# A gated MLP on one core: three single gate loads and their matmuls ahead of all value columns, and one output block stored whole

## The chip, the core and the metric

The kernel runs on one core of one Trainium2 chip. A core has five engines that run side by side: TensorE (PE; its weight loads are listed apart as PEld), VectorE (DVE), ScalarE (ACT), GpSimd (POOL) and SyncE (SP). SP issues most of the DMAs; ACT and POOL can issue DMAs too. Each engine works through its own list of instructions in order, and waits on semaphores where an instruction needs another engine's result or a DMA's landing.

The metric is the device time of one execution in microseconds (us). Lower is better.

## The reference

```python
batch, seq, dim, hidden = 16, 256, 512, 2048
x  = randn(batch, seq, dim)      # 4096 rows of 512, float32
w1 = randn(dim, hidden * 2)      # gate columns, then value columns
w2 = randn(hidden, dim)

def reference(x, w1, w2):
    h = x @ w1
    gate, value = split(h, 2, axis=-1)
    h = maximum(gate, 0) * value
    return (h @ w2).astype(float32)
```

So there are two large matrix products, with a product of the positive part of the gate and the value between them.

## The kernel before

**Stages.** The 4096 rows of x are worked in four sets of 1024 (`SET`), each set in two halves of 512 (`TH`). The hidden dimension of 2048 is cut into 16 blocks of 128 (`jb`, 0 to 15). For each set, the first matrix product makes `g`, the gated hidden values in fp16, block by block, and the second product (`mm2_stream`) multiplies `g` with w2. Both products use a scheme with seven products of halves (`P1` to `P7` in class `Block` and in `mm2_stream`) in place of eight; sums of halves of x, w1, g and w2 are made for it on DVE and POOL. The order of instructions on every engine is the order in which the program emits them (`manual_schedule`); no scheduler changes it.

**The start.** The sums of w1 aren't there yet when the first set starts. So the first three blocks (`NPLAIN = 3`) are computed plainly, by class `Plain`: four matmuls for the gates (`gates`), four for the values (`values`), and `close`, which scales the values on ACT (L269) and multiplies them with the positive part of the gates on DVE (L270). For the first 512 rows (`whole`) a block is one piece of 512 columns; for the second 512 rows (`parts`) it is two pieces of 256.

All that the plain blocks need is loaded by SP in one queue, in the order of the program (L418 to L425): the first 512 rows of x in two loads into `xf`, the gate columns of blocks 0 and 1 in one load, their value columns in one load, rows 512 to 767 of x (`xg[:2]`), the gate columns of block 2, its value columns, and rows 768 to 1023 (`xg[2:]`). `fetch_wl(jb, g_, n)` loads `n` blocks of columns of one kind (`g_` 0 is gate, 1 is value) in float32: 256 KB a block, in rows of 512 bytes a block. `cast_w(jb, g_)` turns one block's columns into fp16 in `wr`, half on ACT and half on DVE (both L401). The loads land in space that belongs to `g` and its sums, so that they cost no memory of their own.

x has to be transposed ahead of the matmuls. `turn_pair` does it for the first 512 rows, in float32, by matmuls with an identity on PE (L383), copied out by DVE (even row blocks) and ACT (odd ones) (L385). The second 512 rows are cast to fp16 on DVE first (`xh`, L459 and L469), then turned by `turn_half` on PE (L391) and copied out on DVE (L392).

**Other work that hangs on these loads.** POOL issues the loads of all other w1 columns, in fp16, and its first one waits behind a small copy (L428) that reads the value columns of block 0: a gate that holds POOL's loads back until those have landed. DVE's first sum of w1 (`w1_one`, L160) needs POOL's first two loads, and `lead`, the first block with seven products (block 3), needs those sums. All SP and ACT loads take their completion semaphores from a ring of eight, so a load waits until the one eight places earlier has landed.

**The end.** In the last set (`last`) the second product's output goes out by block of 128 rows, `b` from 0 to 3, for each half of the set's rows. The upper rows' output `o1` (L324) is stored whole for blocks 0 and 1 and as two halves of 256 columns for blocks 2 and 3. The lower rows' output `o2` is stored in halves for blocks 2 and 3 (L330, L338), and the very last half is issued by ACT (L335).

Of the kernel before, what the change touches and what calls it, by code (L numbers as in the profile page):

```python
# [21 lines left out]
NPLAIN = 3  # L22
# [3 lines left out]
HALF = 256  # L26
# [3 lines left out]
@with_exitstack  # L30
def kernel(ctx: ExitStack, tc: tile.TileContext, x, w1, w2, out):

    nc = tc.nc
    x2 = x.flatten_outer_dims()
    out2 = out.flatten_outer_dims()  # L40
    flagpool = ctx.enter_context(tc.tile_pool(name="flagpool", bufs=1))
    flag = flagpool.tile([1, 1], dt.int32, name="flag")
    with ExitStack() as fast:
        unfit = fast_way(fast, tc, x2, w1, w2, out2, flag)
    with tc.If(unfit > 0, label="general"):
        with ExitStack() as general:
            general_way(general, tc, x2, w1, w2, out2)
# [52 lines left out]
def fast_way(ctx, tc, x2, w1, w2, out2, flag):  # L100
# [4 lines left out]
    H, DO = w2.shape  # L105
# [13 lines left out]
    psy = ctx.enter_context(tc.tile_pool(name="psy", bufs=3, space=bass.MemoryType.PSUM))  # L119
# [164 lines left out]
    def mm2_stream(s, go):  # L284
        last = s == NS - 1
        S = {}

        def mm(name, b, ps, fresh):
            vn, gn = WX[name]
            for k in range(NHC):  # L290
                nc.tensor.matmul(ps, go[gn][:, k, b * P:(b + 1) * P], V[vn][:, k, :], start=fresh and k == 0,  # L291
                                 stop=k == NHC - 1, skip_group_check=True)
                if k < NHC - 1:
                    yield

        def take(pool, nm):
            return pool.tile([P, TH], F32, name=nm, tag=nm)[:, :HALF]

        def step(name, b):
            d = S.setdefault(b, {})  # L300
            if name == "P1":
                d["X"] = take(psx, "X")
                yield from mm("P1", b, d["X"], True)
                d["Y"] = take(psy, "Y")
                nc.scalar.copy(out=d["Y"], in_=d["X"])
            elif name == "P5":
                d["W"] = take(psw, "W")
                yield from mm("P5", b, d["W"], True)
                t = tmp.tile([P, 2, TH], F32, name="pv", tag="tmp")
                d["pu"], d["o2"] = t[:, 0].rearrange("p (a n) -> p a n", a=2), t[:, 1]  # L310
                nc.scalar.activation(d["pu"][:, 0], d["W"], COPY, scale=1 / GS)
            elif name == "P2":
                yield from mm("P2", b, d["X"], False)
                d["o1"] = tmp.tile([P, DO], F32, name="o", tag="o", bufs=4)
                nc.scalar.activation(d["o1"][:, :HALF], d["X"], COPY, scale=1 / GS)
            elif name == "P6":
                yield from mm("P6", b, d["Y"], False)
                nc.scalar.activation(d["pu"][:, 1], d["Y"], COPY, scale=-1 / GS)
            elif name == "P3":
                yield from mm("P3", b, d["W"], False)  # L320
                nc.vector.scalar_tensor_tensor(out=d["o1"][:, HALF:], in0=d["W"], scalar=1 / GS, in1=d["pu"][:, 1],  # L321
                                               op0=MULT, op1=ADD)
                for n in (slice(0, HALF), slice(HALF, DO)) if last and b >= 2 else (slice(0, DO),):
                    nc.sync.dma_start(out=out_v[s, 0, b, :, n], in_=d["o1"][:, n])  # L324
            elif name == "P7":
                yield from mm("P7", b, d["Y"], False)
                nc.vector.scalar_tensor_tensor(out=d["o2"][:, HALF:], in0=d["Y"], scalar=-1 / GS, in1=d["pu"][:, 0],
                                               op0=MULT, op1=ADD)
                if last and b >= NB - 2:
                    nc.sync.dma_start(out=out_v[s, 1, b, :, HALF:], in_=d["o2"][:, HALF:])  # L330
            else:
                yield from mm("P4", b, d["Y"], False)
                nc.scalar.activation(d["o2"][:, :HALF], d["Y"], COPY, scale=1 / GS)  # L333
                if last and b == NB - 1:
                    nc.scalar.dma_start(out=out_v[s, 1, b, :, :HALF], in_=d["o2"][:, :HALF])  # L335
                else:
                    n = slice(0, HALF if last and b == NB - 2 else DO)
                    nc.sync.dma_start(out=out_v[s, 1, b, :, n], in_=d["o2"][:, n])  # L338
            yield

        order = [("P1", 0), ("P1", 1), ("P1", 2), ("P2", 0), ("P2", 1), ("P2", 2)]
        order += [(n, b) for n in ("P5", "P6", "P3", "P7", "P4") for b in (0, 1)]
        order += [("P1", 3), ("P5", 2), ("P2", 3), ("P5", 3)]
        order += [(n, b) for n in ("P6", "P3", "P7", "P4") for b in (2, 3)]
        for i, (n, b) in enumerate(order):
            for f in BESIDE.get((s, i), ()):
                f()
            yield from step(n, b)
# [38 lines left out]
    def turn_half(o, b0, copy):  # L387
        ps = psx.tile([P, 4, 2, P], F16, name="X", tag="X")
        for b in range(2):
            for e in range(4):  # L390
                nc.tensor.transpose(ps[:, e, b], xh[:, b0 + b, e * P:(e + 1) * P], ident[F16])  # L391
        copy(out=o["A2"][:, :, b0 * P:(b0 + 2) * P], in_=ps.rearrange("p e b t -> p e (b t)"))  # L392
# [5 lines left out]
    def cast_w(jb, g_):  # L398
        c, i = place[jb]
        for es, copy in ((slice(0, 2), nc.scalar.copy), (slice(2, 4), nc.vector.tensor_copy)):  # L400
            copy(out=wr[c][:, es, g_, i * P:(i + 1) * P], in_=wl[c][:, es, g_, i * P:(i + 1) * P])  # L401

    def fetch_wl(jb, g_, n=1):
        c, i = place[jb]
        nc.sync.dma_start(out=wl[c][:, :, g_, i * P:(i + n) * P], in_=w1_v[:, :, g_, jb * P:(jb + n) * P])
# [11 lines left out]

    for b in (0, 2):  # L418
        nc.sync.dma_start(out=xf[:, b:b + 2], in_=x_v[0, :, b:b + 2])  # L419
    fetch_wl(0, 0, 2)  # L420
    fetch_wl(0, 1, 2)
    nc.sync.dma_start(out=xg[:, :2], in_=x_v[0, :, NB:NB + 2])
    fetch_wl(2, 0)
    fetch_wl(2, 1)
    nc.sync.dma_start(out=xg[:, 2:], in_=x_v[0, :, NB + 2:])  # L425
    for t in ident.values():
# [7 lines left out]
    whole = [Plain(g, jb, xo["A1"], 0, 0, 2) for jb in range(NPLAIN)]  # L434
# [19 lines left out]
    cast_w(1, 0)  # L454
    whole[0].gates((1,))
    whole[1].gates(None, psy, "Y")
    cast_w(0, 1)
    cast_w(1, 1)
    nc.vector.tensor_copy(out=xh[:, :2], in_=xg[:, :2])  # L459
    whole[0].values()  # L460
    whole[0].close()
    whole[1].values()
    cast_w(2, 0)
    turn_half(xo, 0, nc.vector.tensor_copy)
    whole[2].gates(None, psy, "Y")
    cast_w(2, 1)
    whole[1].close()
    whole[2].values()
    nc.vector.tensor_copy(out=xh[:, 2:], in_=xg[:, 2:])  # L469
# [69 lines left out]
    for s in range(NS):  # L539
# [7 lines left out]
        last = NJ * PERIOD  # L547
# [16 lines left out]
        for at in range(first * PERIOD, last + PERIOD):  # L564
            if at in plan:
                jb, n = plan[at]
# [87 lines left out]
```

## Time and profile before

| what | value |
|---|---|
| median of 3 runs | 309.1 us (309.0 to 309.37) |
| the profiled execution's own time | 309.1 us |
| span of its profile, first to last instruction | 307.3 us |
| mean granted TensorE clock | 0.999 |
| DMA, mean over the span | 103 GB/s |
| longest groups on PE: L205 (first product, seven products) X, Y, W | 379 ns a matmul of 128x512 |
| PE L291 (second product) | 273 ns a matmul of 128x256 |

A line of the timeline reads: start and duration in us, engine, line of the kernel, operation, out<-in by the program's names, size, number of instructions that were merged, and in square brackets the idle time of the engine just ahead and what ended it. The name of a tile is that of the memory it lies in: `g_S<-in_x_dram` is a load of x, `g<-in_w_dram` one of the first three blocks' columns, and `wr<-g` their cast. An "q" behind an engine's name is its queue: an instruction that issues a DMA. Matmuls are pipelined, so a group's end overlaps the next one's start: it is the distance of the starts that counts.

### The profile page before, as it was taken

Reading aid. Unit: us, or ns where it says so; the run is one execution under the profiler, and the core shown is the slowest. Engines: PE = TensorE matmul, PEld = TensorE weight load, DVE = VectorE, ACT = ScalarE, POOL = GpSimd, SP = SyncE. Lnnn points to the kernel's source line nnn. Section 1 sums busy time; section 2 is a strip of 40 time slices with the busy share of each in tenths; the row PEclk is TensorE's granted clock in tenths of the full one; section 3 lists DMA queues with packets and bytes.
Section 4 is the critical chain, followed back from the end, with each engine's and each line's share of the span. In section 5 each row is a group of like instructions: output and inputs, shape, how many; then the busy total and the mean of one; then the engine's idle time right before and its main releaser. Section 6 shows DMA issues by size and latency. Waiting matters only on the chain.

```text
span 307.3 us, 5116 instructions
## 1 busy us (share of the span) xinstructions
PE 300.6 (98%) x1868; PEld 182.7 (59%) x1868; DVE 219.1 (71%) x346; ACT 189.8 (62%) x457; POOL 139.7 (45%) x127
## 2 busy tenths in 40 slices
PE   7999999999999999999999999999999999999994
PEld 4574444588844444488864444458884444448883
DVE  1798898896568888884348888885526888888401
ACT  2557776568576676737856767656857767673230
POOL 1749999810004438990002345994000433898000
PEclk9999999999999999999999999999999999999999
DMA  6999986989615740065130010036321100000123
GB/s 227 305 204 205 207 203 192 183 155 186 237 61 102 140 102 1 2 119 155 69 139 24 11 34 2 0 69 140 138 80 59 34 9 27 0 2 0 69 88 124
DMA packets 34410, 31.54 MB, mean 103 GB/s; under 512 B 14448, under 2 KB 28784, under 8 KB 34160
## 3 DMA queue, kind: packets, MB, share of 16 engines
q1 hardware_dynamic: 24608, 20.32, 21.9%
q0 software_dynamic: 9104, 10.75, 21.3%
q8 instruction: 15, 0.25, 0.4%
q10 hardware_dynamic: 672, 0.13, 0.2%
q14 instruction: 11, 0.09, 0.1%
HBM read 24.12 MB, written 11.53 MB: 116 GB/s over the span
## 4 chain that ended last, share of the span: by engine, by line
PE 96%; DMA 2%; ACT 0%; SPq 0%; issue 0%; ACTq 0%
PE Y L205 26%; PE X L205 17%; PE W L205 17%; PE Y L291 14%; PE W L291 9%; PE X L291 9%; DMA g<-in_w_dram 2%; PE W L255 2%; PE X L255 1%; PE Y L255 1%; SPq L419 0%; PE X L391 0%; ACT Y L212 0%; ACT wr L401 0%; ACT pv L333 0%
## 5 line engine op out<-in xcount | busy, mean ns | idle before, releaser
L280 POOL TENSOR_TENSOR g_S<-g 128x512 f16<-128x512 f16 (+1 forms) x46 | 58.1, 1292 | 126.3 <-DVE g L244 126.3
L205 PEld LDWEIGHTS <-wt 128*128 128x128 f16 x488 | 47.7, 98 | 55.9 <-issue 0.3
L205 PE MATMUL X<-x_A,wr 128*128 128x512 f16 x244 | 72.6, 379 | 0.1
L205 PE MATMUL Y<-x_S,wt 128*128 128x512 f16 x244 | 72.6, 379 | 0.0
L205 PEld LDWEIGHTS <-wr 128*128 128x128 f16 x366 | 35.8, 98 | 41.4 <-issue 0.4
L232 DVE SCALAR_TENSOR_TENSOR cc<-W,pu 128x512 f32<-128x512 f32 x61 | 42.2, 691 | 24.2 <-ACT pu L226 24.2
L212 ACT COPY Y<-X 128x512 f32<-128x512 f32 x61 | 34.8, 570 | 38.0 <-PE X L205 37.5
L291 PEld LDWEIGHTS <-g_S 128*128 128x128 f16 x512 | 50.0, 98 | 5.8
L238 DVE SCALAR_TENSOR_TENSOR cc<-Y,pu 128x512 f32<-128x512 f32 x61 | 42.2, 691 | 6.2
L226 ACT ACTIVATE pu<-Y 128x512 f32<-128x512 f32 x61 | 36.4, 596 | 13.8 <-PE Y L205 13.8
L233 DVE SCALAR_TENSOR_TENSOR g<-X,cc 128x512 f16<-128x512 f32 x61 | 42.2, 691 | 2.4
L244 DVE SCALAR_TENSOR_TENSOR g<-Y,cc 128x512 f16<-128x512 f32 x61 | 41.5, 681 | 1.8 <-PE Y L205 1.8
L291 PEld LDWEIGHTS <-g 128*128 128x128 f16 x384 | 37.6, 98 | 8.2
L219 ACT ACTIVATE pu<-W 128x512 f32<-128x512 f32 x61 | 36.7, 602 | 0.3 <-PE W L205 0.3
L205 PE MATMUL Y<-x_A,wt 128*128 128x512 f16 x122 | 36.3, 379 | 0.0
L205 PE MATMUL W<-x_S,wr 128*128 128x512 f16 x122 | 36.3, 379 | 0.0
L205 PE MATMUL W<-x_S,wt 128*128 128x512 f16 x122 | 36.3, 379 | 0.0
L291 PE MATMUL X<-w,g 128*128 128x256 f16 x256 | 31.2, 273 | 0.0
L291 PE MATMUL Y<-v,g_S 128*128 128x256 f16 x256 | 30.6, 273 | 0.0
L321 DVE SCALAR_TENSOR_TENSOR o<-W,pv 128x256 f32<-128x256 f32 x16 | 6.8, 424 | 29.2 <-PE W L291 29.2
L280 POOL TENSOR_TENSOR g_S<-g,g_S 128x512 f16<-128x512 f16 x18 | 21.8, 1209 | 1.4
L280 POOL TENSOR_TENSOR g_S<-g_S,g 128x512 f16<-128x512 f16 x18 | 20.8, 1154 | 1.4
(76 smaller groups left out, 285.7 us busy)
## 6 DMA issues: line engine op xcount, KB each, us to landing
out_dram<-o SPq DMA_DIRECT2D x14, 256.0 KB, 2.1
out_dram<-pv SPq DMA_DIRECT2D x14, 256.0 KB, 2.0
x<-in_x_dram POOLq DMA_DIRECT2D x3, 1024.0 KB, 9.4
xn<-x SPq DMA_DIRECT2D x12, 256.0 KB, 3.0
g_S<-in_x_dram SPq DMA_DIRECT2D x4, 512.0 KB, 6.5
wr<-in_w_dram POOLq DMA_DIRECT2D x4, 512.0 KB, 13.0
w<-in_w_dram POOLq DMA_DIRECT2D x4, 512.0 KB, 15.4
g<-in_w_dram SPq DMA_DIRECT2D x2, 512.0 KB, 6.5
```

Source lines behind the costliest of these rows:

```text
L205: nc.tensor.matmul(ps, W(wn, self.jb)[:, b], self.xo[xn][:, b, :], start=fresh and b == 0, stop=b == 1, skip_group_check=True)
L212: nc.scalar.copy(out=self.Y, in_=self.X)
L219: nc.scalar.activation(self.p5, self.W, COPY, scale=GS)
L226: nc.scalar.activation(self.u2, self.Y, COPY, scale=-GS)
L232: nc.vector.scalar_tensor_tensor(out=self.c12, in0=self.W, scalar=GS, in1=self.u2, op0=MULT, op1=ADD)
L233: nc.vector.scalar_tensor_tensor(out=self.g[:, self.jb, :TH], in0=self.X, scalar=0.0, in1=self.c12, op0=MAX, op1=MULT)
L238: nc.vector.scalar_tensor_tensor(out=self.c22, in0=self.Y, scalar=-GS, in1=self.p5, op0=MULT, op1=ADD)
L244: nc.vector.scalar_tensor_tensor(out=self.g[:, self.jb, TH:], in0=self.Y, scalar=0.0, in1=self.c22, op0=MAX, op1=MULT)
L255: nc.tensor.matmul(ps[:, ts], W(names[e // 2], self.jb)[:, e % 2], self.a[:, e, ts], start=e == 0, stop=e == 3, skip_group_check=True)
L280: eng.tensor_tensor(go[n][:, h0:h1], go[i0][:, h0:h1], go[i1][:, h0:h1], op=op)
L291: nc.tensor.matmul(ps, go[gn][:, k, b * P:(b + 1) * P], V[vn][:, k, :], start=fresh and k == 0, stop=k == NHC - 1, skip_group_check=True)
L321: nc.vector.scalar_tensor_tensor(out=d["o1"][:, HALF:], in0=d["W"], scalar=1 / GS, in1=d["pu"][:, 1], op0=MULT, op1=ADD)
```

## The change

It has three parts. In the loads, the pair of gate columns (blocks 0 and 1) becomes two single loads, and the gate columns of block 2 follow at once as a third, ahead of the value columns of blocks 0 and 1; before, they came after the rows 512 to 767 of x. In the order of the work, the cast and the gate matmuls of block 2 move ahead of the casts of the values of blocks 0 and 1, and the cast of block 2's values moves ahead of the first `turn_half`, where the cast of block 2's gates was. At the end, the upper output of block 2 is stored whole; only block 3's is stored in halves.

```diff
@@ in mm2_stream
-                for n in (slice(0, HALF), slice(HALF, DO)) if last and b >= 2 else (slice(0, DO),):
+                for n in (slice(0, HALF), slice(HALF, DO)) if last and b >= 3 else (slice(0, DO),):
                     nc.sync.dma_start(out=out_v[s, 0, b, :, n], in_=d["o1"][:, n])
@@ the loads
     for b in (0, 2):
         nc.sync.dma_start(out=xf[:, b:b + 2], in_=x_v[0, :, b:b + 2])
-    fetch_wl(0, 0, 2)
+    for jb in range(NPLAIN):
+        fetch_wl(jb, 0)
     fetch_wl(0, 1, 2)
     nc.sync.dma_start(out=xg[:, :2], in_=x_v[0, :, NB:NB + 2])
-    fetch_wl(2, 0)
     fetch_wl(2, 1)
     nc.sync.dma_start(out=xg[:, 2:], in_=x_v[0, :, NB + 2:])
@@ the plain blocks
     cast_w(1, 0)
     whole[0].gates((1,))
     whole[1].gates(None, psy, "Y")
+    cast_w(2, 0)
+    whole[2].gates(None, psy, "Y")
     cast_w(0, 1)
     cast_w(1, 1)
     nc.vector.tensor_copy(out=xh[:, :2], in_=xg[:, :2])
     whole[0].values()
     whole[0].close()
     whole[1].values()
-    cast_w(2, 0)
+    cast_w(2, 1)
     turn_half(xo, 0, nc.vector.tensor_copy)
-    whole[2].gates(None, psy, "Y")
-    cast_w(2, 1)
     whole[1].close()
     whole[2].values()
     nc.vector.tensor_copy(out=xh[:, 2:], in_=xg[:, 2:])
```

## The prediction

> **What bounds the kernel now.** I read the busy shares and the chain of the page first, then the start and the end of the timeline, engine by engine.
>
> ```profile
> PE 300.6 (98%) x1868; PEld 182.7 (59%) x1868; DVE 219.1 (71%) x346; ACT 189.8 (62%) x457; POOL 139.7 (45%) x127
> ...
> PE 96%; DMA 2%; ACT 0%; SPq 0%; issue 0%; ACTq 0%
> ```
>
> PE carries 96% of the chain that ends last. So whatever makes PE start later, or stand, in the first 25 us is added to the end, and nothing else is. PE in the start:
>
> ```profile
> 7.12 1.04 PE L383 MATMUL X<-ident,g_S 128*128 128x128 f32 x8
> 8.45 1.10 PE L255 MATMUL X<-x_A,wr 128*128 128x256 f16 x8 [0.29 <-ACT wr L401]
> 9.39 1.03 PE L255 MATMUL Y<-x_A,wr 128*128 128x512 f16 x4
> 10.25 1.89 PE L255 MATMUL W<-x_A,wr 128*128 128x512 f16 x8
> 11.98 0.61 PE L391 MATMUL X<-ident,g_S 128*128 128x128 f16 x8
> 12.42 1.07 PE L255 MATMUL Y<-x_A,wr 128*128 128x512 f16 x4
> 13.33 1.03 PE L255 MATMUL W<-x_A,wr 128*128 128x512 f16 x4
> 14.20 0.60 PE L255 MATMUL X<-x_A,wr 128*128 128x256 f16 x4
> ...
> 15.07 0.61 PE L391 MATMUL X<-ident,g_S 128*128 128x128 f16 x8
> ```
>
> X and Y here are gates, W are values. From 8.45 on each group starts when the one before has issued: a 512-wide group of four takes 0.86 (9.39 to 10.25), the eight fp16 transposes of L391 take 0.44, gates and values of a half block 0.87. The only idle time left is the 0.29 ahead of 8.45, and a few hundredths at 8.94 and 12.89. Now the engines that feed these groups, ACT and DVE:
>
> ```profile
> 7.10 0.59 ACT L385 CAST x_A<-W 128x512 f16<-128x512 f32 x1 [4.49 <-PE W L383]
> 7.99 0.40 ACT L401 CAST wr<-g 128x256 f16<-128x256 f32 x1 [0.30 <-DMA g<-in_w_dram]
> 8.30 0.58 ACT L385 CAST x_A<-X 128x512 f16<-128x512 f32 x1
> 9.47 0.71 ACT L401 CAST wr<-g 128x256 f16<-128x256 f32 x2 [0.29 <-DMA g<-in_w_dram]
> ...
> 11.31 0.60 ACT L269 ACTIVATE v<-W 128x512 f32<-128x512 f32 x1 [1.13 <-PE W L255]
> ```
>
> ```profile
> 10.87 0.69 DVE L459 CAST g_S<-g_S 128x1024 f16<-128x1024 f32 x1 [0.90 <-DMA g_S<-in_x_dram]
> 11.94 0.69 DVE L270 SCALAR_TENSOR_TENSOR g<-X,v 128x512 f16<-128x512 f32 x1 [0.38 <-ACT v L269]
> 12.55 0.28 DVE L401 CAST wr<-g 128x256 f16<-128x256 f32 x1
> 12.75 0.68 DVE L392 COPY x_A<-X 128x1024 f16<-128x1024 f16 x1
> 13.35 0.28 DVE L401 CAST wr<-g 128x256 f16<-128x256 f32 x1
> 13.57 0.69 DVE L270 SCALAR_TENSOR_TENSOR g<-Y,v 128x512 f16<-128x512 f32 x1
> 14.18 0.68 DVE L469 CAST g_S<-g_S 128x1024 f16<-128x1024 f32 x1
> ```
>
> Casts that wait for a DMA tell when a load landed: gates of blocks 0 and 1 at 7.99, their values at 9.47, rows 512 to 767 of x at 10.87; the ACT cast of block 2's values starts at 12.63, after a DMA wait. And from 11.94 DVE has no pause: block 0's product, two casts, the copy of the transposed rows (L392), block 1's product, the cast of the last rows (L469), which ends at 14.86. The transposes at 15.07 need that cast: 0.21 to spare, and no more.
>
> **The change, part by part.**
>
> *Loads.* The pair of gates (512 KB) took 7.99 to 9.47 as its twin did for the values: 1.48. Two single loads of 256 KB landed between 10.87 and 12.63: 0.88 each. Three singles cost 2.64 in place of one pair, 1.16 more, until the third, which was to come later anyway, is deducted: 0.28 from there on. So gates 0 land at 7.99 - 1.48 + 0.88 = 7.39; gates 1 at 8.27; gates 2 at 9.15; the value pair at 9.47 + 1.16 = 10.63; rows of x at 12.03; block 2's values at 12.63 + 0.28 = 12.91; the last rows, wanted on DVE from 14.18 on, 0.28 later than now. Bounds of a single: 0.74, half the pair by bytes (values at 10.21), and 1.48, if rows of 512 B cost as much as rows of 1 KB (values at 12.43). I take 0.88, which is the same load in the same queue.
>
> The Trainium skill, page "DMA: Bandwidth & Descriptors", section Bandwidth (measured for loads issued from GpSimd), speaks against splitting: it fits some 2.0 us fixed per DMA and says to batch to 1 MiB. By it three loads of 256 KB would be an estimated 7.8 us if they ran one after another, values would land some 6 us late, and the kernel would lose about 5 us. The rows above, 0.88 between two landings of 256 KB on SP's queue, do not agree: the fixed part overlaps inside the queue.
>
> *The first gates.* The cast of gates 0 waits no more for 7.99 but for ACT, free at 7.10 + 0.59 = 7.69; it is done at 8.09, and PE, done with its transposes at 8.16, starts at once in place of 8.45. But the second half of the first block needs the copy of the last transposed rows (ACT, 8.30 now), which can't start before those transposes end: 8.19 to 8.78, then PE at 8.83 in place of 8.94. So 0.11 is gained, not 0.29.
>
> *Gates 1, 2, then values.* PE: second half 8.83, gates 1 at 9.27, gates 2 at 10.14, values 0 wanted at 11.00. Casts for gates 1 and 2 are done by about 9.2 and 9.6. Values land at 10.63; ACT cast 0.40, hand-over 0.05: 11.08, so PE stands 0.08 (at a single's 0.74 the values would be ready at 10.66: none). Total PE work is the same, one group of gates has only changed places; it costs 0 by itself.
>
> *What the move makes late.* DVE's chain hangs on the end of values 0. ACT takes them 1.06 after their start (10.25 to 11.31), DVE's product follows 0.63 later: 11.08 + 1.69 = 12.77, where it was 11.94. Behind it in DVE's order, by the starts above: product 0.61, one cast now instead of two 0.20, copy of the transposed rows 0.60, block 1's product 0.61, cast of the last rows 0.68. So that copy runs 13.58 to 14.26, and the last cast 14.79 to 15.47. PE: values 0 at 11.08, values 1 at 11.94, transposes 12.81, values 2 at 13.25, first half block of the second 512 rows wanted at 14.12, but its x is ready at 14.26 + 0.06 = 14.32: 0.20 of waiting. The second transposes are then wanted at 14.32 + 0.87 = 15.19 and wait for 15.47 + 0.06 = 15.53: 0.34. Against 15.07 PE is 0.46 late; with cheap singles (values 0 at 11.00) 0.38. The gain of 0.11 is in these figures.
>
> What is late next: the product of block 2 and the first half block, then the copy behind the second transposes, 16.34 to 17.02, needed at 15.53 + 0.44 + 4 x 0.44 = 17.73: covered by 0.65. From there DVE waits for ACT's values, which follow PE (now 17.01, after a wait of 0.30), so everything moves together and the later PE stall on DVE (L205 at 24.80, 0.17) stays what it is. Nothing gives the delay back: PE is full up to its end.
>
> *POOL.* Its copy at L428 waits for the value pair, so its eight loads are issued 1.16 later. The first two feed DVE's L160 at 17.35 (17.81 after the change): issued at 9.75 and 10.68, 5.6 to landing, that is about 16.3 for the second, 17.5 later: hidden by 0.3. Should the cover go, each 0.1 is a 0.1 on DVE ahead of the sums that Block 3 needs.
>
> *SP's queue.* One issue more in front. Completion semaphores rotate, so block 2's values wait for the small load `first` (4.3 us from 0.83, i.e. 5.1) where they were issued at 4.2, and the last rows wait for the first x to land (about 5.4) and were issued at 5.57. Both move no byte before 10: nothing.
>
> *The end.*
>
> ```profile
> 302.94 0.38 ACT L333 ACTIVATE pv<-Y 128x256 f32<-128x256 f32 x1 [0.49 <-PE Y L291]
> 303.35 0.37 ACTq L335 DMA_DIRECT2D out_dram<-pv  x1
> ```
>
> The last DMA leaves at 303.35, 2.2 to landing. Block 2's first output half went out at 293.81 and now goes with the second half at 299.08, as one DMA, 256 KB (2.1 to landing in the rows of such DMAs: 301.2). It would have to be over 4 us slower to count. SP has one issue of 0.33 less, and its next ones wait for DVE. Zero.
>
> **Sum.** Profiled execution: 309.1, of which the span is 307.3; the median of the runs is 309.1 too. 309.1 + 0.38 to 0.46: 309.5.
>
> **Rivals.**
>
> (a) Single loads cost more than 0.88. Each 0.01 on a single puts the values 0.03 later, and all of it goes on. From 0.93 a single, 6% more, the loss passes 0.62; at 1.00 the values land at 10.99, values 0 start at 11.44, second transposes at 15.89: +0.82, 309.9; at 1.48 it would be 311.3. For it: three stand in a row ahead of everything; a missed POOL cover would add to it. Against: the two singles measured ran while POOL was issuing, which the first three won't.
>
> (b) The other side: DVE isn't late, because its order is shorter than I read it (one cast less, overlaps), or the last rows' cast slips in earlier. Then the 0.11, at most the 0.29 ahead of 8.45, stands: 308.8 to 309.0. It decides only if the cast of the last rows ends by 14.90; with 2.70 us of DVE work behind a product that can't start before 12.69, it ends at 15.39. Speaks for it: nothing in the rows.
>
> (c) The loads don't land as counted and gain and loss cancel: 309.1. That takes values 0 at 10.6, earlier than PE can get there.
>
> **How the numbers follow.** A measurement of this kernel tells about 0.2% (0.62 us) from no change. Forecast 0.64, its own range 309.2 to 309.9, with 0.20 of it over 309.72; (a) 0.22, all over 309.72; (b) 0.10, half of it below 308.48 by scatter or by something that I don't see at the end; (c) 0.04. Slower 0.42, same 0.53, faster 0.05. The range 309.0 to 310.2 leaves out most of (b) and the far part of (a), some 0.16.
>
> **What would show it.** Right: PE's first group at about 8.2 with a pause of some 0.2 inside the first block, value matmuls from 11.0 to 11.1, waits on DVE ahead of the half block near 14.3 and of the L391 transposes near 15.5, and all later PE groups of block 3 some 0.4 later. Wrong: an ACT cast of the values that starts after 10.8 (a), L391's second group before 15.2 (b), DVE's L160 waiting for a DMA (POOL's cover), or a last landing that isn't L335's.

## The result, and the profile after

The changed kernel took 310.14 us in the median of six runs (310.11 to 311.32), the kernel before 309.04 (308.9 to 309.37). The ratio of the means is 1.0043, with a 95% interval of 1.0028 to 1.0058: slower by 1.1 us in the median and 1.3 in the mean, where 0.4 was predicted. The profiled execution took 310.14, of which the span is 308.2 (309.1 and 307.3 before).

The page of the changed kernel, busy shares and chain. DVE and ACT have 1% of the chain each now, and PE 93% where it had 96%:

```profile
PE 300.4 (97%) x1868; PEld 181.7 (59%) x1868; DVE 219.4 (71%) x346; ACT 190.0 (62%) x457; POOL 139.5 (45%) x127
...
PE 93%; DMA 2%; DVE 1%; SPq 1%; ACT 1%; issue 0%; ACTq 0%
```

The timeline of its PE:

```profile
6.61 1.06 PE L383 MATMUL X<-ident,g_S 128*128 128x128 f32 x8
7.94 1.10 PE L255 MATMUL X<-x_A,wr 128*128 128x256 f16 x8 [0.26 <-ACT wr L401]
8.87 1.89 PE L255 MATMUL Y<-x_A,wr 128*128 128x512 f16 x8
11.20 1.90 PE L255 MATMUL W<-x_A,wr 128*128 128x512 f16 x8 [0.44 <-ACT wr L401]
12.94 0.61 PE L391 MATMUL X<-ident,g_S 128*128 128x128 f16 x8
13.45 1.19 PE L255 MATMUL W<-x_A,wr 128*128 128x512 f16 x4
14.63 0.60 PE L255 MATMUL X<-x_A,wr 128*128 128x256 f16 x4
...
15.92 0.62 PE L391 MATMUL X<-ident,g_S 128*128 128x128 f16 x8 [0.26 <-DVE g_S L469]
```

PE starts its gates 0.51 earlier than before (7.94, not 8.45) and works off all three blocks' gates. Then it has nothing to do: the eight matmuls from 8.87, 0.216 apart, are issued by 10.60, and the values start at 11.20. The half block starts at 14.63 (14.20 before), the second transposes at 15.92 (15.07). From there on PE's groups stand in line again, and its last matmul starts 0.86 later than before (303.49 and 302.63). That holds beyond these two runs: in 13 of the 14 traces of this case PE's last matmul starts 287.54 to 287.56 after the second transposes (287.42 in e10 below). So what is late at the second transposes is late at the end, by the same amount.

What it waits for is told by the chain that ended last, in order of time, from the load of the values to those transposes (start, duration, what; "issue" is time in which the engine waited for nothing that the profile shows):

```profile
3.70 7.02 DMA g<-in_w_dram
10.71 0.02 issue
10.74 0.41 ACT wr L401
11.15 0.05 issue
11.20 1.05 PE W L255 x4
12.25 0.02 issue
12.27 0.61 ACT v L269
12.88 0.02 issue
12.90 0.69 DVE g L270
13.60 0.39 DVE wr L401
13.98 0.59 DVE x_A L392
14.57 0.60 DVE g L270
15.17 0.70 DVE g_S L469
15.87 0.05 issue
15.92 0.62 PE X L391 x8
```

This is the predicted chain link by link: the value pair lands at 10.71, ACT casts, PE multiplies, ACT scales, DVE makes block 0's product, casts, copies, makes block 1's product and casts the last rows, and only then PE may transpose them. In the kernel before, the chain runs from the load of the first gates over their cast on ACT to PE, and from 8.45 on it stays on PE up to the last matmul: neither the values' load nor DVE was in it.

### The profile page after: what moved, and what is told of

It reads as the page before. It is cut to its first block, busy times and chain, and to the rows that moved or that the text cites. A ratio compares the mean times of both kernels' runs of the same rounds, so it can differ in the third digit from the quotient of the medians.

```text
span 308.2 us, 5117 instructions
## 1 busy us (share of the span) xinstructions
PE 300.4 (97%) x1868; PEld 181.7 (59%) x1868; DVE 219.4 (71%) x346; ACT 190.0 (62%) x457; POOL 139.5 (45%) x127
## 4 chain that ended last, share of the span: by engine, by line
PE 93%; DMA 2%; DVE 1%; SPq 1%; ACT 1%; issue 0%; ACTq 0%
PE Y L205 26%; PE X L205 17%; PE W L205 17%; PE Y L291 14%; PE W L291 9%; PE X L291 9%; DMA g<-in_w_dram 2%; PE W L255 1%; PE X L255 1%; SPq L405 1%; DVE g L270 0%; SPq L419 0%; DVE g_S L469 0%; PE X L391 0%; ACT v L269 0%
```

## The experiments

There were three batches of four kernels. "Before" is the kernel before, run on the same chip in the same batch, always with its eight warm-up matmuls (matmuls on zeros, L177, that PE does while the first loads are under way); "warm" means ten of them in place of eight. The interval is that of the ratio of the means. All times in us.

| run | best | median | before, best and median | ratio, 95% interval |
|---|---|---|---|---|
| e1 end alone | 309.12 | 310.16 | 309.01, 309.50 | 0.9994 to 1.0035 |
| e2 pair again | 309.66 | 310.34 | the same | 1.0004 to 1.0034 |
| e3 singles alone | 310.14 | 310.96 | the same | 1.0013 to 1.0053 |
| e4 last cast first | 309.32 | 310.15 | the same | 0.9999 to 1.0030 |
| e5 before, warm | 308.94 | 309.25 | 309.00, 309.59 | 0.9970 to 0.9997 |
| e6 changed, warm | 309.86 | 310.24 | the same | 1.0005 to 1.0038 |
| e7 singles, same count | 309.26 | 310.13 | the same | 0.9989 to 1.0028 |
| e8 one store more | 310.06 | 310.40 | the same | 1.0016 to 1.0054 |
| e9 last cast first, warm | 309.29 | 309.45 | 308.91, 309.19 | 0.9992 to 1.0020 |
| e10 DVE freed, warm | 308.81 | 309.18 | the same | 0.9986 to 1.0013 |
| e11 POOL later, warm | 309.73 | 309.90 | the same | 1.0011 to 1.0030 |
| e12 loads alone, warm | 309.97 | 310.18 | the same | 1.0019 to 1.0044 |

### First batch: which part, and is it the single loads

e1, the end alone:

```diff
-... if last and b >= 2 else (slice(0, DO),):
+... if last and b >= 3 else (slice(0, DO),):
```

> The kernel before with only the change at the end (block 2's upper output stored whole). Theory M (the gate matmuls moved ahead delay values 0 and, through DVE, the second transposes): the end costs nothing, 309.0 to 309.2 us, last landing is that of L335, PE's last matmul starts within 0.1 of 302.6. Rival T (the later, larger store holds up the end): over 309.3 us.

e2, the changed kernel with a pair of gates:

```diff
-    for jb in range(NPLAIN):
-        fetch_wl(jb, 0)
+    fetch_wl(0, 0, 2)
+    fetch_wl(2, 0)
     fetch_wl(0, 1, 2)
```

> The changed kernel with its order of work, but the gates of blocks 0 and 1 loaded as one pair again, then block 2's, then the values. Theory M: pair lands near 8.0, block 2's gates 8.9, values 10.4, values 0 start at 10.9 to 11.1 in place of 11.20, DVE chain behind them as long as before, second transposes at 15.6 to 15.9: 309.8 to 310.1 us. Rival S (the single loads with their 512-byte rows are the loss): 309.0 to 309.3 us.

e3, the kernel before with single loads:

```diff
-    fetch_wl(0, 0, 2)
+    fetch_wl(0, 0)
+    fetch_wl(1, 0)
     fetch_wl(0, 1, 2)
```

> The kernel before with its order of work, but the gates of blocks 0 and 1 as two single loads. Theory M: first gates land at 7.4, values at 9.8, values 0 start at 10.2 to 10.4 (10.25 before), the second transposes at 15.0 to 15.2 (15.07 before): 308.9 to 309.3 us. Rival S: most of the loss, 309.8 us or more.

e4, the changed kernel with the last cast ahead:

```diff
+    nc.vector.tensor_copy(out=xh[:, 2:], in_=xg[:, 2:])
     whole[1].close()
     whole[2].values()
-    nc.vector.tensor_copy(out=xh[:, 2:], in_=xg[:, 2:])
```

> The changed kernel with one move on DVE: the cast of the last rows of x goes ahead of block 1's product. Theory M: that cast starts at 14.4 to 14.5 and ends at 15.2, the second transposes start at about 15.5 (15.92 in the changed kernel) and PE ends 0.4 earlier: 309.6 to 309.8 us. Rival S, or any cause in the loads: no change, 310.1 us.

The times decide little, because all of them scatter by 1.3 to 2.6 us on this chip, the kernel before too (309.01 to 311.3). The traces show a reason. PE's first transposes in the profiled run of e1, from its timeline:

```profile
5.66 1.94 PE L383 MATMUL W<-ident,g_S 128*128 128x128 f32 x8 [0.79 <-DMA g_S<-in_x_dram]
7.39 0.63 PE L177 MATMUL Y<-warm 128*128 128x512 f16 x1
7.82 1.91 PE L383 MATMUL X<-ident,g_S 128*128 128x128 f32 x8
9.53 1.48 PE L255 MATMUL X<-x_A,wr 128*128 128x256 f16 x8
```

Eight transposes take 1.91 where the changed kernel's took 1.06, and eight half matmuls 1.48 where they took 1.10: PE runs at half rate up to about 10 us. The trace's record of the granted clock says the same: full rate is granted from 10.15 on in e1, from 6.60 in the kernel before, 3.94 in the changed one and 10.27 in e4. The start of e1 is that of the kernel before, yet its second transposes start 1.61 later (16.68 and 15.07), and its last matmul starts 1.60 later. So a run's time depends on when PE reaches full rate, and the four medians of this batch are no measure of 0.4 us. The Trainium skill, page "TensorE: Matmul & The Clock Gate", section "Part 1: The HAM clock gate", has full rate come after a busy window of some 3.4 us that runs freely and isn't tied to the kernel's start, and has its moment vary by 500 ns either way. The traces agree with the window: in all 14 the stretch at full rate is 296.96, 300.37 or 303.79 us long, so it goes in steps of 3.41. They don't agree with the 500 ns: the moment lies anywhere from 3.94 to 10.27.

What is read inside the traces stands. e2: values 0 at 11.18, just over the 10.9 to 11.1 of theory M, and second transposes at 15.62, as expected under M; the best run, 309.66, lies between the two theories. Most of the loss stays without the single loads of blocks 0 and 1: 0.55 of 0.85 at the second transposes.

e1: 4.62 us from PE's last matmul's start to the end of the span, 4.68 before; best run 0.11 over the best before. Its last matmul starts at 304.23, not within 0.1 of 302.6, for the late full rate. The end shows no cost, but no time pins that closer than some 0.3.

e3 missed both ways: its second transposes start at 15.38 (15.07 before, 15.0 to 15.2 expected), which is 0.3, and its end is longer, 5.87 from PE's last matmul instead of 4.68. No theory had foreseen that, and it is taken up below.

e4 decided nothing: with full rate from 10.27 on, PE came to the values only at 12.43 and to the second transposes at 16.53 (about 15.5 expected), behind its own work and not behind DVE's, and the median was 310.15 (309.6 to 309.8 expected). The same edit comes back as e9.

### Second batch: less scatter, and the long end

e5 and e6, the kernel before and the changed one:

```diff
-NWARM = 8
+NWARM = 10
```

> The kernel before with ten warm-up matmuls in place of eight, so that PE is not idle between them and the first transposes. Theory R (part of the scatter of the kernel before, 309.0 to 311.3 us, is the moment when PE goes to full rate: 6.6 us in one trace, 10.2 in another): full rate by 7 us in the trace, nearly all runs 309.0 to 309.5 us. Rival: the scatter has another cause and stays, a third of the runs over 309.8 us.

> The changed kernel with ten warm-up matmuls. Theory M (values 0 late, DVE chain behind them): full rate early changes nothing of the waits, values 0 start at 11.1 to 11.3, second transposes at 15.6 to 16.0, 309.9 to 310.3 us, 0.8 to 1.1 over the kernel before with ten. Theory R alone (the loss is a matter of when PE reaches full rate): the same as the kernel before with ten, within 0.2.

e7, single loads with as many DMAs as before (e3 and e1 together):

```diff
-    fetch_wl(0, 0, 2)
+    fetch_wl(0, 0)
+    fetch_wl(1, 0)
...
-... if last and b >= 2 else (slice(0, DO),):
+... if last and b >= 3 else (slice(0, DO),):
```

> The kernel before with the gates of blocks 0 and 1 as single loads, and block 2's upper output stored whole, so that the number of DMAs is again that of the kernel before. Theory E (the 1.2 us longer end of the run with single loads alone comes from the place of the last DMA's semaphore in the list that SP waits through at the end): 4.6 to 4.8 us from PE's last matmul's start to the end, as in the kernel before, best runs 309.1 to 309.4. Rival S (single loads cost by themselves): best runs 310.0 us or more.

e8, one store more, with the start of before:

```diff
-... if last and b >= 2 else (slice(0, DO),):
+... if last and b >= 1 else (slice(0, DO),):
```

> The kernel before with one store more at the end (block 1's upper output in halves too); nothing changed in the start. Theory E: the last DMA's semaphore becomes the first in SP's list, the other seven waits come behind it, the end is 0.5 to 1.2 us longer (5.2 to 5.9 from PE's last matmul's start), best runs 309.6 to 310.2. Rival: one store more costs only its issue, which is covered: best runs 309.0 to 309.2.

e5: all twelve runs lie between 308.94 and 309.81, nine of them at 309.5 or below, and the transposes take 1.06, as theory R has it. It is the one version whose interval against the kernel before lies below 1: 0.9983, 0.9970 to 0.9997. Its best run is 0.06 under the best before, so the gain is that late runs are missing, not a faster start. Ten warm-ups don't end all scatter: e6, e10 and e12 have single runs of 310.67 to 311.19, and no trace shows what those met.

e6: values 0 at 11.09, second transposes at 15.82, median 0.99 and best run 0.92 over e5's. So the loss is in the change, not in the moment of full rate.

e7 and e8 show that the long end belongs to the number of DMAs. With the count of before, e7 has 4.54 from the last matmul's start to the end; e8, untouched in the start, 5.74. SP's own waits from 302 us on, the kernel before and then e8 (line, releaser: total, times, longest):

```profile
SPq L45 <- SPq L45: 2.4, 4, 1.4
```

```profile
SPq L45 <- SPq L45: 2.7, 1, 2.7
```

At the end SP waits for eight completion semaphores in a fixed order. Before, it passes the early ones while the last store is still under way, and the last store's comes near the end of the list. With one DMA more, the last store has the first semaphore in the list: one wait of 2.7, and the other seven are gone through behind it. Best runs are 1.06 (e8) and 1.13 (e3) over those of before; e3's trace has 0.29 of that on PE. Its end of 5.87 is 1.19 longer than before: the waits behind the last landing make 0.53 of it, the last store landed 2.41 after its issue in place of 2.25, and SP's steps behind the list took 2.12 in place of 1.61. Why these last steps took longer is open.

### Third batch: where on DVE, and what the loads do alone

All four have ten warm-ups. e9 is e4's edit on the changed kernel:

```diff
+    nc.vector.tensor_copy(out=xh[:, 2:], in_=xg[:, 2:])
     whole[1].close()
     whole[2].values()
-    nc.vector.tensor_copy(out=xh[:, 2:], in_=xg[:, 2:])
```

> The changed kernel with ten warm-up matmuls and DVE's cast of the last rows ahead of block 1's product. Theory M: values 0 start at 11.1 as with ten warm-ups alone, the second transposes at 15.4 in place of 15.82, 0.4 us off: best runs near 309.45 us, median near 309.8. If DVE's order isn't what holds the transposes: as with ten warm-ups alone, best 309.86, median 310.24.

e10 adds to e9:

```diff
-    cast_w(2, 1)
+    for es in (slice(0, 2), slice(2, 4)):
+        nc.scalar.copy(out=wr[1][:, es, 1], in_=wl[1][:, es, 1])
```

> As the one before, and block 2's value columns are cast wholly by ACT, so that DVE's chain behind block 0's product is one copy and one cast. Theory M: no wait at the half block, second transposes at 15.0 to 15.2, as in the kernel before with ten warm-ups: best runs 309.0 to 309.2 us, median 309.2 to 309.5. If late values cost by themselves (PE 0.3 of waiting at 11.1 goes on to the end), 0.3 or more over that.

e11, on the changed kernel:

```diff
     nc.gpsimd.tensor_copy(out=gate, in_=wl[0][:, 0, 1, :1])
+    nc.gpsimd.tensor_copy(out=gate, in_=wl[0][:, 0, 1, :1])
```

> The changed kernel with ten warm-up matmuls and POOL's small copy done twice, so that its loads are issued 0.3 us later. Theory P (DVE's cast of block 2's values takes 0.47 in place of 0.28 because it meets a certain part of a POOL issue, 0.4 to 0.6 after its start): the cast takes 0.28 and the second transposes start 0.1 to 0.3 earlier than 15.82. Rival (its length comes from what it reads and writes): 0.47 again, no change.

e12, the kernel before with the loads and the end of the changed one:

```diff
-    fetch_wl(0, 0, 2)
+    for jb in range(NPLAIN):
+        fetch_wl(jb, 0)
     fetch_wl(0, 1, 2)
     nc.sync.dma_start(out=xg[:, :2], in_=x_v[0, :, NB:NB + 2])
-    fetch_wl(2, 0)
...
-... if last and b >= 2 else (slice(0, DO),):
+... if last and b >= 3 else (slice(0, DO),):
```

> The loads and the end of the changed kernel with the order of work of the kernel before (block 2's gates after the first transposes of the second 512 rows), ten warm-up matmuls. Theory M in its part on loads: values 0 can't start before 11.1 (10.2 with ten warm-ups and the loads of before), PE waits there 0.9 to 1.2 with nothing in between, second transposes at 15.8 to 16.0, best runs 309.8 to 310.0 us: the order of the loads alone costs what the whole change does. Rival (the order of work costs, the loads don't): 309.0 to 309.3.

e9: second transposes at 15.38, 0.44 behind the values ahead of them and without a wait for DVE (e6: 15.82, with a wait of 0.26 for it); best run 0.38 over the best before, where e6 had 0.86. From its timeline of PE:

```profile
14.94 0.60 PE L255 MATMUL W<-x_A,wr 128*128 128x256 f16 x4
15.38 0.61 PE L391 MATMUL X<-ident,g_S 128*128 128x128 f16 x8
```

e10: the timeline of its PE,

```profile
11.29 1.89 PE L255 MATMUL W<-x_A,wr 128*128 128x512 f16 x8
13.02 0.61 PE L391 MATMUL X<-ident,g_S 128*128 128x128 f16 x8
13.49 1.04 PE L255 MATMUL W<-x_A,wr 128*128 128x512 f16 x4
14.41 0.60 PE L255 MATMUL X<-x_A,wr 128*128 128x256 f16 x4
14.84 0.60 PE L255 MATMUL W<-x_A,wr 128*128 128x256 f16 x4
15.28 0.61 PE L391 MATMUL X<-ident,g_S 128*128 128x128 f16 x8
```

The second transposes follow the values by 0.44, as in the kernel before, and the time is back: median 309.18 against 309.19. (They start at 15.28, not at 15.0 to 15.2, because this run had full rate only from 7.12 on, its first gates started at 8.35 and its values at 11.29; PE doesn't wait for them. Its last matmul is nevertheless only 0.07 later than before, because a wait of 0.30 that the other 13 traces have on PE near 164 us is missing in this one; why is open.) So with two small moves on DVE these runs show no cost of the gate order against the kernel before, and no gain either. It was not run beside e5, and the kernel before had eight warm-ups here, so whether the gate order costs anything against e5 isn't shown.

e12, the loads alone, timeline of PE:

```profile
8.82 1.03 PE L255 MATMUL Y<-x_A,wr 128*128 128x512 f16 x4
11.17 1.90 PE L255 MATMUL W<-x_A,wr 128*128 128x512 f16 x8 [1.32 <-ACT wr L401]
```

PE waits 1.32 for the values with nothing in between (0.9 to 1.2 expected); the second transposes start at 16.19, 0.2 later than expected, and the best run is 1.06 over the best before. The order of the loads alone costs what the whole change does. The new order of work fills part of that hole with block 2's gates, but doesn't hand DVE its first product any sooner.

e11 failed as a test. DVE's cast took 0.48 again, but POOL's third load was issued 0.39 before it, exactly as in e6: the delay, 0.23 in the trace, was swallowed by a shorter second issue (0.95, not 1.18). Theory P is neither shown nor refuted by it. Its rival, though, falls with e2. There the same cast stands between the same two instructions on DVE and reads and writes the same, and it took 0.28; the changed kernel's line, and then e2's:

```profile
13.51 0.47 DVE L401 CAST wr<-g 128x256 f16<-128x256 f32 x1
```

```profile
13.48 0.28 DVE L401 CAST wr<-g 128x256 f16<-128x256 f32 x1
```

## Where the prediction was right, and the step that failed

*The loads* were priced right. Gates landed at 7.46, 8.34 and 9.23 (7.39, 8.27, 9.15 predicted), 0.88 and 0.89 apart; values at 10.71 (10.63). Rival (a), dear single loads, is out: that took 0.93 or more. The prediction puts both of its points from the Trainium skill, page "DMA: Bandwidth & Descriptors", under section Bandwidth; the rule on batching stands there, but the fit of 2.0 us per DMA stands in the section "Anatomy of one DMA — SWDGE (gpsimd) path". The landings 0.88 apart again don't agree with it.

*The first gates* came sooner than predicted (7.94 and 8.43, not 8.16 and 8.83), because PE had reached full rate by 3.9 us and transposed faster. That was luck of the run, not the change: in e4, with the same loads, they started at 9.39. It gained nothing: the prediction had PE stand 0.08 ahead of the values, it stood 0.60. A start that ends in a wait for a DMA buys only a longer wait.

*What the move makes late* named the right chain, both waits (half block 14.32 predicted, 14.63 measured; second transposes 15.53, 15.92) and that nothing gives it back. The step that failed is the size of DVE's chain and of the wait ahead of it: the sum gave 0.38 to 0.46 for what was 0.85 at the second transposes and 0.86 at PE's last matmul. Four terms were too small:

- "values 0 at 11.08": 11.20, 0.08 of it landing, 0.04 cast and hand-over.
- "one cast now instead of two 0.20": 0.39 in the chain, as the cast took 0.47 and not 0.28. This is half of the whole error.
- "cast of the last rows 0.68", with its hand-over 0.74: 0.83 from 15.10 to 15.92.
- ACT and DVE behind the values, 1.69: 1.71, less 0.02 in the steps between.

Together 0.39, which is the gap between 15.53 and 15.92. e2 shows that the chain itself was read rightly: there the cast took 0.28, and from the values to the second transposes it was 4.44 (11.18 to 15.62), where the prediction's terms add up to 4.45; in the changed kernel it was 4.72. The rest of the way from 0.46 to the measured 1.1: the profiled span grew by 0.94, the end after PE's last matmul being 4.76 long in place of 4.68, and the medians moved 0.16 more than the spans, within what runs of one kernel differ by.

The second error is in the odds: the sum was made of rows of one trace, in which both casts of block 2 on DVE took 0.28, and nothing in its range stood for a longer one. The largest chance, 0.53, went to "within 0.2%"; it was slower.

*SP's queue and the end* were put at zero, and as a pair they are: one load more in front, one store less behind. Taken singly one of them isn't: with a DMA more, the end was 1.19 (e3) and 1.06 (e8) longer in the traces. The prediction saw that semaphores rotate, but looked only at the waits ahead of loads, not at SP's last list.

*POOL's cover* held: DVE's first sum of w1 waited for no DMA. POOL's second load landed at 16.93, not at the 17.5 of the prediction (16.44 before): issued 1.27 later, it came only 0.49 later. Rival (b) fell with DVE's order as read, rival (c) with values at 11.20.

## What to carry to other kernels

Ahead of a queue of loads, ask of each one who waits for what it delays: here the earliest gates were cheap to have and the values 1.26 later paid for them, since a chain through ACT, PE and DVE hangs on the values. Where PE is the bound, an early start is worth only what the next wait leaves of it; look for the second engine (DVE here) whose order turns one late input into two late outputs, and move the urgent cast ahead of the product that can wait. And keep the count of DMAs in mind when a load is split: in this program the list of semaphores at the end is part of the time.

## What the runs showed of the hardware

PE's full rate came at 3.9 to 10.3 us in the eight traces of kernels with eight warm-up matmuls, which leave PE idle for 0.6 to 1.0 ahead of the first transposes; in four of them it came at 9.7 or later. With ten, which leave it idle for 0 to 0.5, it came by 7.1 in all six traces. That the idle time is the reason was not tested by itself.

DVE's casts of block 2's columns (128x256) took 0.28 twelve times in the traces, and 0.43 to 0.48 eight times. In each of the eight, a POOL issue of a load had begun 0.38 to 0.46 before the cast; in each of the twelve, 0.03 to 0.20 or 0.65 to 0.70 before it. POOL's issues take 0.75 to 0.79 as a rule (the first 0.94), but 1.1 to 1.2 where a long DVE cast of x starts 0.1 to 0.2 into them (the second issue in the changed kernel, 11.95 to 13.12, over the cast from 12.13 to 12.82). The Trainium skill, page "SBUF — State Buffer", section "Who interferes with whom", says that DVE casts in a two-port mode and GpSimd share a pair of ports by an exclusive lock, so that whoever comes second stands still for the whole of the other's instruction. Both kinds of long row agree with that, one for each side as the loser. The five casts that began 0.03 to 0.20 into a POOL issue don't: they took 0.28, so the whole issue doesn't block. No row shows in which mode the casts ran, and no run here separates the lock from other causes, e11 having missed.
